# One change to the chunked recurrence of a hybrid decoder block: three short groups of products per chunk become one

## The chip, the core and the metric

The kernel runs on one core of a Trainium2 chip. The metric is device time in microseconds (us) of one execution; a profiled execution leaves a trace with the start and length of every instruction. PE is the matrix engine (TensorE), PEld its weight loads, DVE the vector engine, ACT the scalar engine, POOL the GpSimd engine, SP the queue that issues most DMA transfers.

## The reference

One decoder layer over 512 tokens with width 1024. An input projection feeds a sparse-attention mixer, an RWKV-7 mixer and two gates; both mixers are projected and merged, and a gated MLP follows. The change is about the RWKV-7 recurrence, which the reference writes as a scan over tokens, for 8 heads with a 64 x 64 state each:

```python
def step(state, inp):
    r_t, w_t, k_t, v_t, a_t, b_t = inp
    sa = jnp.einsum('bhij,bhj->bhi', state, a_t)
    state = state * w_t[:, :, None, :] + sa[..., None] * b_t[:, :, None, :] + v_t[..., None] * k_t[:, :, None, :]
    return state, jnp.einsum('bhij,bhj->bhi', state, r_t)
...
mean = jnp.mean(y, axis=-1, keepdims=True)
var = jnp.mean(jnp.square(y - mean), axis=-1, keepdims=True)
y = (y - mean) * lax.rsqrt(var + GN_EPS) * ln_g.reshape(H, N) + ln_b.reshape(H, N)
y = y + jnp.sum(r * k * r_k, axis=-1, keepdims=True) * v
return y.reshape(b, s, RWKV_WIDTH) * g
```

Two further parts are touched: the columns of the input projection that make the gates (`sigmoid(gate_a)`, `sigmoid(gate_b)`), and the compression MLP of the attention mixer, whose last product gives `vc`.

## The kernel before

**The recurrence in chunks.** The 512 tokens are cut into `NCH` = 8 chunks of `C` = 64. Heads are held in pairs: `p` counts 4 pairs, `r` the two heads of a pair, in the lower and upper 64 partitions. The loop over `c` (L930) works out, for each chunk:

- `X`, a PSUM bank: the chunk's own term (`x_own`, L917, eight products on a 64 x 64 tile of the array) plus `AR . M0`, the state's part (eight products, L935). `Xs` is its copy to SBUF (L941, DVE).
- `U` (L946): eight products of `AB` with `Xs`. Two copies put it into `UV`: ACT the lower partitions (L947), DVE the upper (L948).
- `Mp` (L957): eight products of `BKT` with `UV`, on a 128 x 64 tile. Two DVE operations add it to the state and scale it by `PC`, giving `M1`, the state of the next chunk.
- `Y`, the output: `AR . M0` (L939, 64 x 64) and `AB . UV` (L968, 128 x 64). ACT copies it to `Ys`; every second chunk, `group_norm` (L849) normalizes two chunks' `Ys` on DVE and ACT, then turns it with transposes on PE, multiplies it with a gate product (`gg`), and puts the result into `BO`.

So `X` to `Xs` to `U` to `UV` to `Mp` is a chain with two hops through DVE and ACT. Each small fp32 product appears in the trace as two matmul records, so eight products read as x16.

**The dense products between.** The generator `fill_chain` (L875) holds other work for PE. One `next(fill)` is one step: 12 of the 24 matmuls of a dense product with 128 columns of weights (`dense_fm_g`, L400: 8 x 2 with the weights' high part `whi` against the activations' two parts `hh` and `hl`, then 8 with the low part `wlo`), or a piece of the compression MLP (`compress`, L784), or one token block of a K/V projection (`kv1`). The loop calls it three times per chunk: after `Xs`, after `UV`, and at the end (L942, L952, L987), and once ahead of the loop. The products for gate A are called GA1 to GA7 here, those for gate B GB0 to GB6.

**Weights.** `wload` (L260) has SP fetch a 512 KB tile into one of three `raw` buffers. `wsplit_` (L277) makes the high part on ACT (L292) and the low part on the engine that `weight_tiles` (L213) names (L294): DVE for most, POOL for some. `whi` and `wlo` have two buffers each, and a `raw` buffer is fetched into again when its low part has been made. The two weight tiles of each piece of the compression MLP use `raw` buffers directly, until PE has read them.

**Order.** PE's order in the recurrence is the program's (`manual_schedule` with PE). The order on ACT, DVE, POOL and SP comes from a planner which runs ahead of time, and each of these engines then takes its instructions strictly in that order. A product that reads or writes a PSUM bank and a copy that reads the same bank are kept apart, by tile.

Of the kernel before, what the change touches and what calls it, by code (L numbers as in the profile page):

```python
# [10 lines left out]
F32 = mybir.dt.float32  # L11
# [3 lines left out]
ALU = mybir.AluOpType  # L15
# [8 lines left out]
DH = 64  # L24
H = 8
NH2 = H // 2
C = 64
NCH = S // C
# [52 lines left out]
def hybrid_block(ctx: ExitStack, tc: tile.TileContext, A: dict, out: bass.AP):  # L81
    nc = tc.nc
    v, sc, te = nc.vector, nc.scalar, nc.tensor
# [19 lines left out]
    def close(cm):  # L103
        cm.__exit__(None, None, None)
# [8 lines left out]
    def pa():  # L113
        return bank("a", 2)
# [4 lines left out]
    def mm(o, l, r, start, stop):  # L119
        te.matmul(o, lhsT=l, rhs=r, start=start, stop=stop)  # L120

    def act(o, i, f=AF.Copy, **kw):
        sc.activation(o, i, f, **kw)  # L123

    def tt(o, a, b, op):
        v.tensor_tensor(o, a, b, op=op)  # L126
# [45 lines left out]
    def cols(name):  # L172
        r0, n = ROWS[name]
        return prm[:, r0:r0 + n]
# [38 lines left out]
    def weight_tiles():  # L213
        def cols(w, o, kt=KT, eng=v):
            return w[:, o:o + 128], kt, 128, eng

        def rows(w, o, n, kt=KT, eng=v):
            step = 1024 // n
            for i, k0 in enumerate(range(0, kt, step)):
                kn = min(step, kt - k0)  # L220
                yield w[128 * k0:128 * (k0 + kn), o:o + n], kn, n, eng[i] if type(eng) is list else eng

        pool_ = nc.gpsimd
        yield cols(w_in, O_RWKV + 1536, eng=pool_)
        yield cols(w_in, O_RWKV + 1664, eng=pool_)
        for p in range(NH2):
            for o in (512, 0, 1024):
                yield cols(w_in, O_RWKV + o + 128 * p)
        yield cols(w_in, O_KC)
        yield from rows(w_in, O_Q, 512, eng=[v, pool_, ("spare", pool_), v])  # L230
        yield cols(w_in, O_VC)
        yield from rows(w_in, O_KS, 256, eng=[v, ("spare", v)])
        for m in range(NGA):
            yield cols(w_in, O_GA + 128 * m)
        yield from rows(w_in, O_KW, 280, eng=pool_)
        for m in range(NGA, KT):
            if m < 4:
                for s4 in range(m if m > NGA else 0, m + 1):
                    for s_ in "kv":
                        yield A["cmp_w1_" + s_][0][512 * s4:512 * s4 + 512], 4, 256, None  # L240
            yield cols(w_in, O_GA + 128 * m)
        for m in range(NGB):
            yield cols(w_in, O_GB + 128 * m)
        for m in range(KT):
            if m + NGB < KT:
                yield cols(w_in, O_GB + 128 * (m + NGB), eng=pool_ if m else v)
            yield cols(A["w_proj_b"][0], 128 * m, NH2, eng=pool_)
        for m in range(KT):
            yield cols(A["w_proj_a"][0], 128 * m, NH2)
        yield from rows(A["w_out"][0], 0, 512)  # L250
        yield from rows(A["w_out"][0], 512, 512, eng=())
        for f in range(NF):
            yield cols(A["w_up"][0], DFF + 128 * f)
            yield cols(A["w_up"][0], 128 * f)
        for hf in range(2):
            yield from rows(A["w_down"][0], 512 * hf, 512, NF)
# [136 lines left out]
    def run(g):  # L393
        while True:
            try:
                next(g)
            except StopIteration as e:
                return e.value

    def dense_fm_g(xh, xl, kt=KT):  # L400
        hi, lo = wnext(kt, 128)
        p = mmb()
        for k in range(kt):
            mm(p, hi[:, k], xh[:, k], k == 0, False)
            mm(p, hi[:, k], xl[:, k], False, False)
            if 4 * k == 3 * kt - 4:
                yield
        for k in range(kt):
            mm(p, lo[:, k], xh[:, k], False, k == kt - 1)
        return p  # L410
# [373 lines left out]
    def compress():  # L784
# [43 lines left out]
        for g in range(2):  # L828
            for e in range(2):
                bs = slice(64 * g + 32 * e, 64 * g + 32 * e + 32)  # L830
                for m in range(2):
                    mm(kc_ps[bs, 128:192], hidT[:, m, 1, 32 * g:32 * g + 32], cw2[:, 1, m], m == 0, m == 1)
                act(vcb[bs, 2 * g + e], kc_ps[bs, 128:192], AF.Copy, scale=0.5)
        for g in range(2):
            act(kcd[:, g, 0], kc_ps[0:32, 64 * g:64 * g + 64], AF.Copy, scale=0.5)
# [39 lines left out]
    def fill_chain():  # L875
        cp_ = compress()
        next(cp_)
        next(kv1)
        yield
        next(cp_)  # L880
        yield from kv1
        ts(gts, gts, 0.25, 0.25)
        yield
        for m in range(NGA, KT):
            next(cp_, None)
            act(siga[m], (yield from dense_fm_g(hh, hl)))
            yield
        assert next(cp_, 0) == 0
        for m in range(NGB):
            act(tb[m], (yield from dense_fm_g(hh, hl)))  # L890
            yield

# [21 lines left out]
    def hsl(r, n=64):  # L914
        return slice(64 * r, 64 * r + n)
# [6 lines left out]
                   c == 0 and p == NH2 - 1)  # L922


    with tc.manual_schedule(engines={mybir.EngineType.PE}):
        M0 = Ys = gn = None
        X = pb()
        x_own(0, X)
        next(fill, None)
        for c in range(NCH):  # L930
            Y = pa()
            if M0 is not None:
                for p in range(NH2):
                    for r in range(2):
                        mm(X[hsl(r), 64 * p:64 * p + 64], AR[hsl(r), p, c, 0, :], M0[hsl(r), p, :], False,  # L935
                           p == NH2 - 1)
                for p in range(NH2):
                    for r in range(2):
                        mm(Y[hsl(r), 64 * p:64 * p + 64], AR[hsl(r), p, c, 1, :], M0[hsl(r), p, :], p == 0, False)  # L939
            Xs = tp.tile([128, NH2, DH], F32, name="Xs", tag="Xs", bufs=2)  # L940
            v.tensor_copy(Xs, X[:, 0:256].rearrange("p (a d) -> p a d", d=DH))  # L941
            next(fill, None)  # L942
            U = pb()
            for p in range(NH2):
                for r in range(2):
                    mm(U[hsl(r), 64 * p:64 * p + 64], AB[hsl(r), c, p, r, 0:64], Xs[hsl(r), p], True, True)  # L946
            act(UV[0:64, c, :, 0, :], U[0:64, 0:256].rearrange("p (a d) -> p a d", d=DH))  # L947
            v.tensor_copy(UV[64:128, c, :, 1, :], U[64:128, 0:256].rearrange("p (a d) -> p a d", d=DH))  # L948
            if c < NCH - 1:
                X = pb()  # L950
                x_own(c + 1, X)
            next(fill, None)  # L952
            if c < NCH - 1:
                Mp = pa()
                for p in range(NH2):
                    for r in range(2):
                        mm(Mp[hsl(r), 64 * p:64 * p + 64], BKT[:, c, p, r, :], UV[:, c, p, r, :], True, True)  # L957
                M1 = tp.tile([128, NH2, DH], F32, name="M", tag="M", bufs=2)
                mpv = Mp[:, 0:256].rearrange("p (a d) -> p a d", d=DH)
                pc = PC[:, :, c:c + 1].to_broadcast([128, NH2, DH])  # L960
                if M0 is None:
                    tt(M1, mpv, pc, ALU.mult)
                else:
                    tt(M1, M0, mpv, ALU.add)
                    tt(M1, M1, pc, ALU.mult)
            for p in range(NH2):
                for r in range(2):
                    mm(Y[hsl(r), 64 * p:64 * p + 64], AB[:, c, p, r, 64:128], UV[:, c, p, r, :],  # L968
                       M0 is None and p == 0, p == NH2 - 1)
            if c % 2 == 0:  # L970
                Ys = tp.tile([128, H, DH], F32, name="Ys", tag="Ys", bufs=2)
            for r in range(2):
                act(Ys[hsl(c % 2), r::2, :], Y[hsl(r), 0:256].rearrange("p (h d) -> p h d", d=DH))
            if c % 2 == 1:
                gn = group_norm(c - 1, Ys)
                if c < NCH - 1:
                    next(gn)
            M0 = M1
            if 4 <= c < 6:
                for a in range(4 * c - 16, 4 * c - 12):  # L980
                    bias_rows(a)
            if c == NCH - 2:
                bias_compressed()
            if c == NCH - 1:
                for h0 in range(0, H, 4):
                    act(BT[:, h0:h0 + 4, 0:256], BT[:, h0:h0 + 4, 256:257].to_broadcast([128, 4, 256]))
            next(fill, None)  # L987
            if gn is not None and c % 2 == 0:
                run(gn)
                gn = None  # L990
    close(rp_cm)


# [383 lines left out]
```

## Time and profile before

| | us |
|---|---|
| median of 3 runs | 848.09 (847.67 to 848.52) |
| the profiled execution | 847.76 |
| its span, first to last instruction | 846.0 |
| busy: PE, PEld, DVE, ACT, POOL | 831.9, 676.2, 514.7, 405.7, 52.5 |
| the recurrence on PE, from x_own(0) to the last copy to Ys | about 180 to 288 |

In the timeline each row has the start (us from the span's start), the length, the engine, the line, the operation, the tiles (out<-in), the tile of the array or the shape, and the count of merged instructions. In brackets stand the engine's idle time before the row and what ended it. L120 is the line of the helper that issues every matmul, L123 that of every ACT operation. "128*128", "64*64" and "128*64" are the part of the array that a product uses. The end of a matmul is modelled, so the pace is read from start to start.

### The profile page before, as it was taken

The numbers are of one execution on the slowest core, as the hardware profiler recorded it, in microseconds if no ns is written. First come the engines' busy times: TensorE is split into PE (matmuls) and PEld (weight loads), VectorE is DVE, ScalarE is ACT, GpSimd is POOL, SyncE is SP. The second block draws the span as 40 slices with busy tenths as digits, with TensorE's granted clock in tenths as the row PEclk, the third lists the DMA queues.
The fourth block names the chain that finished last, engine by engine and source line by source line (L and its number), as shares of the span: only waits on it lengthen the run. The fifth ranks groups of instructions, "written<-read, shape, count | busy, mean of one in ns | idle before, by whom it ended". The sixth has DMA issues, their size and how long they took to land.

```text
span 846.0 us, 12844 instructions
## 1 busy us (share of the span) xinstructions
PE 831.9 (98%) x5097; PEld 676.2 (80%) x5097; DVE 514.7 (61%) x998; ACT 405.7 (48%) x784; POOL 52.5 (6%) x69
## 2 busy tenths in 40 slices
PE   7999999999999999999999999999999999999998
PEld 6777778897777886777788888888888888888886
DVE  5477779963555678888675566666666666322222
ACT  6766645443545677767344454444444444221210
POOL 6200020140000110111000000000000000000000
PEclk9999999999999999999999999999999999999999
DMA  7432222335551320010167023333333332333421
GB/s 231 112 86 62 75 75 76 92 108 151 132 119 50 83 69 13 15 36 26 52 215 221 0 77 98 100 100 100 100 100 95 90 91 98 100 100 112 136 75 50
DMA packets 109104, 78.73 MB, mean 93 GB/s; under 512 B 3869, under 2 KB 97748, under 8 KB 109044
## 3 DMA queue, kind: packets, MB, share of 16 engines
q1 hardware_dynamic: 106512, 73.51, 29.8%
q0 software_dynamic: 1472, 1.86, 1.0%
q10 hardware_dynamic: 1060, 2.55, 1.0%
q8 instruction: 40, 0.66, 0.3%
q14 instruction: 20, 0.16, 0.1%
HBM read 74.56 MB, written 2.29 MB: 91 GB/s over the span
## 4 chain that ended last, share of the span: by engine, by line
PE 52%; DVE 0%; ACT 0%; DVEq 0%; issue 0%
PE ps_mm L120 52%; DVE hl L135 0%; PE ps_a L120 0%; PE ps_b L1181 0%; PE ps_a L200 0%; PE ps_mm L1181 0%; ACT hh L123 0%; PE ps_b L200 0%; DVE x L126 0%; DVEq L1373 0%; PE ps_a L1133 0%
## 5 line engine op out<-in xcount | busy, mean ns | idle before, releaser
L294 DVE TENSOR_TENSOR wlo<-raw,whi 128x1024 fp32r<-128x1024 f32 (+1 forms) x111 | 131.6, 1185 | 189.4 <-PE ps_mm L120 166.8
L120 PE MATMUL ps_mm<-hh,whi 128*128 128x512 f32 (+1 forms) x624 | 243.3, 392 | 0.4 <-ACT hh L123 0.3
L120 PE MATMUL ps_mm<-hl,whi 128*128 128x512 f32 (+1 forms) x624 | 240.9, 388 | 0.3 <-DVE hl L135 0.2
L123 ACT ACTIVATE whi<-raw 128x1024 fp32r<-128x1024 f32 (+3 forms) x124 | 123.4, 996 | 170.3 <-PE ps_mm L120 142.4
L120 PE MATMUL ps_mm<-hh,wlo 128*128 128x512 f32 (+1 forms) x624 | 151.8, 385 | 0.0
L120 PEld LDWEIGHTS ps_mm<-hh,whi 128*128 128x128 f32 x624 | 117.3, 188 | 27.3 <-issue 1.3
L120 PEld LDWEIGHTS ps_mm<-hl,whi 128*128 128x128 f32 x624 | 117.4, 188 | 24.1 <-DVE hl L135 1.0
L120 PEld LDWEIGHTS ps_mm<-hh,wlo 128*128 128x128 f32 x624 | 115.2, 188 | 23.3
L120 PE MATMUL ps_mm<-whi,aT 128*128 128x512 f32 x352 | 84.5, 390 | 0.0
L120 PEld LDWEIGHTS ps_mm<-whi,aT 128*128 128x128 f32 x352 | 65.9, 188 | 14.3 <-issue 0.4
L135 DVE SCALAR_TENSOR_TENSOR cgv<-ps_mm,cw,cgv 128x511 f32<-128x511 f32 (+1 forms) x88 | 65.4, 746 | 1.5
L123 ACT ACTIVATE cgv<-ps_mm,cw 128x512 f32<-128x512 f32 x44 | 34.3, 781 | 22.8 <-PE ps_mm L120 22.8
L120 PE MATMUL ps_mm<-wlo,aT 128*128 128x512 f32 x176 | 44.3, 390 | 0.0
L123 ACT ACTIVATE P<-P,nm 128x512 f32<-128x512 f32 (+3 forms) x64 | 35.4, 554 | 14.9 <-DVE nm L1155 14.9
L123 ACT ACTIVATE aT<-cgv 128x512 fp32r<-128x512 f32 x22 | 13.9, 631 | 56.8 <-DVE cgv L126 56.8
L120 PEld LDWEIGHTS ps_mm<-wlo,aT 128*128 128x128 f32 x176 | 33.1, 188 | 6.9
L123 ACT ACTIVATE cgv<-cgv 128x512 f32<-128x512 f32 x22 | 13.9, 632 | 43.9 <-DVE cgv L135 43.8
L294 POOL TENSOR_TENSOR wlo<-raw,whi 128x512 fp32r<-128x512 f32 (+3 forms) x13 | 20.4, 1573 | 203.6 <-PE ps_mm L120 147.9
L1155 DVE CUSTOM_DVE_ANT_0 P<-ps_a,AB 128x512 f32<-128x512 f32 (+3 forms) x64 | 29.4, 484 | 4.2 <-PE ps_a L120 3.7
L126 DVE TENSOR_TENSOR x<-x,ps_mm 128x512 f32<-128x512 f32 (+1 forms) x17 | 11.1, 656 | 23.9 <-PE ps_mm L120 22.7
L126 DVE TENSOR_TENSOR aT<-cgv,aT 128x512 fp32r<-128x512 f32 x22 | 15.2, 693 | 14.7 <-ACT aT L123 14.7
L120 PE MATMUL ps_a<-KH,qst 128*128 128x512 f32 (+3 forms) x64 | 21.3, 349 | 1.5 <-DVE nm L1155 0.9
(356 smaller groups left out, 1205.5 us busy)
## 6 DMA issues: line engine op xcount, KB each, us to landing
raw<-in_w_up_dram SPq DMA_DIRECT2D x44, 512.0 KB, 3.8
raw<-in_w_in_dram SPq DMA_DIRECT2D x38, 512.0 KB, 3.9
raw<-in_w_down_dram SPq DMA_DIRECT2D x22, 512.0 KB, 3.6
raw<-in_w_out_dram SPq DMA_DIRECT2D x8, 512.0 KB, 3.7
xt<-in_x_dram SPq DMA_DIRECT2D x4, 512.0 KB, 5.7
raw<-in_cmp_w_k_dram SPq DMA_DIRECT2D x4, 512.0 KB, 4.0
raw<-in_cmp_w_v_dram SPq DMA_DIRECT2D x4, 512.0 KB, 4.4
raw<-in_w_proj_b_dram SPq DMA_DIRECT2D x8, 256.0 KB, 2.7
```

What stands on the lines that cost most here:

```text
L120: te.matmul(o, lhsT=l, rhs=r, start=start, stop=stop)
L123: sc.activation(o, i, f, **kw)
L126: v.tensor_tensor(o, a, b, op=op)
L135: v.scalar_tensor_tensor(o, a, s, b, op0=op0, op1=op1)
L294: eng.tensor_tensor(lo, raw, hi.bitcast(F32), op=ALU.subtract)
L1155: v.tensor_tensor_reduce(out=P[:, i], in0=sp[:, N * (i - i0):N * (i - i0) + N], in1=BT[:, h, 384 - 128 * qt:512], scale=-1.0, scalar=-NEG, ...
```

## The change

- In the loop, the output of chunk c-1 (`outputs`, new) is computed in chunk c, in two halves: the state's part and two head pairs between `X` and `U`, the other two pairs between `U` and the own term of the next chunk. The last chunk's output follows its own `U`.
- `x_own` of the next chunk and `Mp` follow directly; only then come the chunk's three steps of `fill`, in one stretch. In chunk 0 one step stays between `Xs` and `U`, in place of the one ahead of the loop.
- `Xs` is copied in two halves of two pairs each, one by DVE, one by ACT.
- `group_norm` of chunks c-2 and c-1 starts in the even chunk c ahead of the stretch, and its transposes follow the stretch.
- The low parts of GA1 to GA7 and GB0 to GB6 are made on POOL in place of DVE (14 tiles).
- In `compress`, the eight products for `vc` are issued together and their four copies (`vcb`) after them, where each pair of products was followed by its copy.
- A check that `compress` has ended is made one product later.

```diff
-            yield cols(w_in, O_GA + 128 * m)
+            yield cols(w_in, O_GA + 128 * m, eng=pool_)
         for m in range(NGB):
-            yield cols(w_in, O_GB + 128 * m)
+            yield cols(w_in, O_GB + 128 * m, eng=pool_)
...
                 for m in range(2):
                     mm(kc_ps[bs, 128:192], hidT[:, m, 1, 32 * g:32 * g + 32], cw2[:, 1, m], m == 0, m == 1)
+        for g in range(2):
+            for e in range(2):
+                bs = slice(64 * g + 32 * e, 64 * g + 32 * e + 32)
                 act(vcb[bs, 2 * g + e], kc_ps[bs, 128:192], AF.Copy, scale=0.5)
...
-        assert next(cp_, 0) == 0
         for m in range(NGB):
+            if m == 1:
+                assert next(cp_, 0) == 0
...
+    def outputs(c, M):
+        Y = pa()
+        for p in range(NH2 if M is not None else 0):
+            for r in range(2):
+                mm(Y[hsl(r), 64 * p:64 * p + 64], AR[hsl(r), p, c, 1, :], M[hsl(r), p, :], p == 0, False)
+        for p in range(NH2):
+            if p == 2:
+                yield
+            for r in range(2):
+                mm(Y[hsl(r), 64 * p:64 * p + 64], AB[:, c, p, r, 64:128], UV[:, c, p, r, :], M is None and p == 0,
+                   p == NH2 - 1)
+        for r in range(2):
+            act(Ys[c // 2][hsl(c % 2), r::2, :], Y[hsl(r), 0:256].rearrange("p (h d) -> p h d", d=DH))
...
-            v.tensor_copy(Xs, X[:, 0:256].rearrange("p (a d) -> p a d", d=DH))
-            next(fill, None)
+            v.tensor_copy(Xs[:, 0:2], pairs(X)[:, 0:2])
+            act(Xs[:, 2:4], pairs(X)[:, 2:4])
+            if c == 0:
+                next(fill, None)
+            else:
+                if c % 2 == 1:
+                    Ys[c // 2] = tp.tile([128, H, DH], F32, name="Ys", tag="Ys", bufs=2)
+                yc = outputs(c - 1, Mp0)
+                next(yc)
             U = pb()
...
+            Mp0 = M0
+            if c:
+                run(yc)
             if c < NCH - 1:
                 X = pb()
                 x_own(c + 1, X)
-            next(fill, None)
-            if c < NCH - 1:
                 Mp = pa()
...
+                M0 = M1
+            else:
+                run(outputs(c, Mp0))
...
-            next(fill, None)
-            if gn is not None and c % 2 == 0:
+            if c and c % 2 == 0:
+                gn = group_norm(c - 2, Ys[c // 2 - 1])
+                next(gn)
+            for i in range(3):
+                next(fill, None)
+            if gn is not None:
                 run(gn)
                 gn = None
+        gn = group_norm(NCH - 2, Ys[NCH // 2 - 1])
```

More of the change, by code (lines that the diff above doesn't have):

```diff
@@ L922, in x_own, with pairs @@
                    c == 0 and p == NH2 - 1)
+    def outputs(c, M):
[11 more added lines that the diff above has]
+            act(Ys[c // 2][hsl(c % 2), r::2, :], Y[hsl(r), 0:256].rearrange("p (h d) -> p h d", d=DH))
+    def pairs(ap):
+        return ap[:, 0:256].rearrange("p (a d) -> p a d", d=DH)
     with tc.manual_schedule(engines={mybir.EngineType.PE}):
-        M0 = Ys = gn = None
+        M0 = M1 = gn = None
+        Ys = {}
         X = pb()
         x_own(0, X)
-        next(fill, None)
         for c in range(NCH):
-            Y = pa()
             if M0 is not None:
@@ L936, in hybrid_block @@
                            p == NH2 - 1)
-                for p in range(NH2):
-                    for r in range(2):
-                        mm(Y[hsl(r), 64 * p:64 * p + 64], AR[hsl(r), p, c, 1, :], M0[hsl(r), p, :], p == 0, False)
             Xs = tp.tile([128, NH2, DH], F32, name="Xs", tag="Xs", bufs=2)
-            v.tensor_copy(Xs, X[:, 0:256].rearrange("p (a d) -> p a d", d=DH))
-            next(fill, None)
+            v.tensor_copy(Xs[:, 0:2], pairs(X)[:, 0:2])
[7 more added lines that the diff above has]
+                next(yc)
             U = pb()
@@ L946, in hybrid_block @@
                     mm(U[hsl(r), 64 * p:64 * p + 64], AB[hsl(r), c, p, r, 0:64], Xs[hsl(r), p], True, True)
-            act(UV[0:64, c, :, 0, :], U[0:64, 0:256].rearrange("p (a d) -> p a d", d=DH))
-            v.tensor_copy(UV[64:128, c, :, 1, :], U[64:128, 0:256].rearrange("p (a d) -> p a d", d=DH))
+            act(UV[0:64, c, :, 0, :], pairs(U)[0:64])
+            v.tensor_copy(UV[64:128, c, :, 1, :], pairs(U)[64:128])
+            Mp0 = M0
+            if c:
+                run(yc)
             if c < NCH - 1:
@@ L958, in hybrid_block @@
                 M1 = tp.tile([128, NH2, DH], F32, name="M", tag="M", bufs=2)
-                mpv = Mp[:, 0:256].rearrange("p (a d) -> p a d", d=DH)
                 pc = PC[:, :, c:c + 1].to_broadcast([128, NH2, DH])
                 if M0 is None:
-                    tt(M1, mpv, pc, ALU.mult)
+                    tt(M1, pairs(Mp), pc, ALU.mult)
                 else:
-                    tt(M1, M0, mpv, ALU.add)
+                    tt(M1, M0, pairs(Mp), ALU.add)
                     tt(M1, M1, pc, ALU.mult)
[L966 to L978, printed above, removed]
+                M0 = M1
+            else:
+                run(outputs(c, Mp0))
             if 4 <= c < 6:
@@ L986, in hybrid_block @@
                     act(BT[:, h0:h0 + 4, 0:256], BT[:, h0:h0 + 4, 256:257].to_broadcast([128, 4, 256]))
-            next(fill, None)
-            if gn is not None and c % 2 == 0:
+            if c and c % 2 == 0:
[4 more added lines that the diff above has]
+            if gn is not None:
                 run(gn)
                 gn = None
+        gn = group_norm(NCH - 2, Ys[NCH // 2 - 1])
     close(rp_cm)
```

## The prediction

> **What bounds the kernel now.** I read the page first, then the chain that ended last, then the timeline of each engine in the recurrence.
>
> ```profile
> span 846.0 us, 12844 instructions
> PE 831.9 (98%) x5097; PEld 676.2 (80%) x5097; DVE 514.7 (61%) x998; ACT 405.7 (48%) x784; POOL 52.5 (6%) x69
> PE 52%; DVE 0%; ACT 0%; DVEq 0%; issue 0%
> ```
>
> PE is busy 98% of the span, and the chain that ended last runs over PE alone. So DVE time that moves to POOL gains nothing by itself. What counts is the sum of PE's issue times and of PE's waits. A busy PE still loses time when it changes the part of the array it uses:
>
> ```profile
> 195.34 0.39 PE L120 MATMUL ps_mm<-hh,whi 128*128 128x512 f32 x1
> 195.57 0.39 PE L120 MATMUL ps_mm<-hl,whi 128*128 128x512 f32 x1
> 195.89 0.68 PE L120 MATMUL ps_b<-M,AR 64*64 64x64 f32 x16
> 196.41 0.63 PE L120 MATMUL ps_a<-M,AR 64*64 64x64 f32 x16
> 196.97 0.50 PE L120 MATMUL ps_mm<-hh,whi 128*128 128x512 f32 x1
> 197.31 0.39 PE L120 MATMUL ps_mm<-hl,whi 128*128 128x512 f32 x1
> ...
> 210.19 0.63 PE L120 MATMUL ps_a<-M,AR 64*64 64x64 f32 x16
> 210.75 1.95 PE L120 MATMUL ps_mm<-raw,sg 128*64 128x256 f32 x16
> ...
> 283.04 0.68 PE L120 MATMUL ps_b<-Xs,AB 64*64 64x64 f32 x16
> 283.65 0.50 PE L120 MATMUL ps_mm<-hh,whi 128*128 128x512 f32 x1
> ```
>
> Dense matmuls follow each other every 0.23 (195.34 to 195.57). One group of 16 records lasts 0.61 to the next shape (283.04 to 283.65), two lasted 1.08 (195.89 to 196.97), so 16 records cost 0.47 in steady flow and the boundary about 0.14: 0.05 in the first 16 (0.52) and 0.09 in the last (0.56). Into a short group PE loses 0.09 more (0.32 against 0.23), and the first dense matmul behind it 0.11 (0.34 against 0.23). A short group between dense stretches thus costs 0.34 beyond its work. The pair at 210.19 is the important one: a change from 64*64 to 128*64 takes the same 0.56 as a change back to dense. I price every inner change of shape at 0.14.
>
> [...]
>
> **Part 1, shapes: +0.2.** Before, chunks 1 to 7 have three short groups each: 3 x 0.34 = 1.02. After, there is one group, but inside it X and the output's state part (64*64), output (128*64), U (64*64), output, own term, Mp alternate: five changes, 0.34 + 5 x 0.14 = 1.04. The saving of two boundaries is eaten. Chunk 0 falls from two groups (0.68) to one with a single change (0.48), -0.20. Pieces of the compression MLP that used to touch a short group move: four weight pieces cost 0 or 0.14 at a touch, 0.34 alone; two gain a neighbour, two lose one, about +0.05, and the last transposes lose theirs, +0.20. With 7 x 0.02 this gives +0.2. Bounds: -4.7 if inner changes were free (7 x 5 x 0.14 = 4.9 less), +0.6.
>
> **Part 2, vcb copies behind all products: -1.4.**
>
> ```profile
> 238.44 0.86 PE L120 MATMUL ps_mm<-QK 128*32 128x64 f32 x12
> 239.60 0.41 PE L120 MATMUL ps_mm<-QK 128*32 128x64 f32 x4 [0.30 <-ACT kc L123]
> 240.32 0.41 PE L120 MATMUL ps_mm<-QK 128*32 128x64 f32 x4 [0.30 <-ACT kc L123]
> 241.03 0.41 PE L120 MATMUL ps_mm<-QK 128*32 128x64 f32 x4 [0.30 <-ACT kc L123]
> ```
>
> Twelve records last 0.86 with a tail near 0.2, so about 0.06 each, and four need 0.24. With the wait for the copy, a group takes 0.72 (239.60 to 240.32). Three waits of 0.47 go; the products run through. The bracket says 0.30 because ends of matmuls are modelled.
>
> **Part 3, the hops.** Today every copy of the recurrence hides behind 12 dense matmuls, 2.8 us. Then about 1 us of short products hides it. The copies:
>
> ```profile
> 183.14 0.28 ACT L123 ACTIVATE QK<-ps_mm 128x128 f32<-128x128 f32 x1 [1.39 <-PE ps_mm L120]
> 188.42 0.43 DVE L948 COPY UV<-ps_b 64x256 f32<-64x256 f32 x1 [6.50 <-ACT UV L123]
> 196.62 0.42 DVE L941 COPY Xs<-ps_b 128x256 f32<-128x256 f32 x1 [1.28 <-PE ps_b L120]
> 245.09 0.38 ACT L123 ACTIVATE UV<-ps_b 64x256 f32<-64x256 f32 x1 [2.55 <-PE ps_b L120]
> ```
>
> DVE's half of UV waited for ACT's half: two copies from one bank run one after the other. The UV hop is therefore 0.22 (a group's tail: 0.68 of rows against 0.46 of starts) + 0.38 + 0.43 + three handovers of 0.05 = 1.2. Its cover in chunks 1 to 6 is two pairs' output (0.24 + 0.14), the own term (0.61) and the change ahead of them (0.14), 1.1: no stall above 0.1 while ACT and DVE are free. Xs, in halves of about 0.28, likewise needs 0.6 for its first half and 0.9 for its second, against a cover of 1.1 and 1.3 (in chunk 1, with no state's part yet, 0.6 and 0.8).
>
> [...]
>
> Stalls where they are not free, or the cover is short:
>
> - Chunk 0, UV hop: the cover is the own term alone, 0.61 against 1.2: +0.6 (0.4 to 0.9, ACT also copies a K/V block then).
> - Chunk 0, loads. The stretch there follows the first weight piece directly.
>
> ```profile
> 184.91 0.40 PE L120 MATMUL ps_mm<-whi,hh 128*128 128x280 f32 x1
> 187.05 0.51 PE L120 MATMUL ps_b<-Xs,AB 64*64 64x64 f32 x10
> 191.08 1.90 PE L120 MATMUL ps_mm<-raw,sg 128*64 128x256 f32 x16
> 192.91 0.50 PE L120 MATMUL ps_mm<-hh,whi 128*128 128x512 f32 x1
> 185.47 0.46 SPq L265 DMA_DIRECT2D raw<-in_w_in_dram  x1
> 190.60 1.06 ACT L123 ACTIVATE whi<-raw 128x1024 fp32r<-128x1024 f32 x1 [1.98 <-DMA raw<-in_w_in_dram]
> ```
>
> The piece ends at 184.91; its buffers let GA1's load start at 185.47, and whi is ready at 191.66, 6.75 later. Without the short groups PE has two K/V blocks (2 x 2.14) and a piece (1.83) ahead of GA1: 6.1. Stall +0.6 (0 to 1.2).
>
> - Chunk 2, the order on ACT: +1.5.
>
> ```profile
> 202.70 0.50 PE L120 MATMUL ps_mm<-hh,whi 128*128 128x512 f32 x1
> 204.60 0.45 SPq L265 DMA_DIRECT2D raw<-in_w_in_dram  x1
> 210.25 1.06 ACT L123 ACTIVATE whi<-raw 128x1024 fp32r<-128x1024 f32 x1 [2.64 <-DMA raw<-in_w_in_dram]
> ...
> 216.75 1.06 ACT L123 ACTIVATE whi<-raw 128x1024 fp32r<-128x1024 f32 x1 [3.37 <-DMA raw<-in_w_in_dram]
> 218.02 0.36 ACT L123 ACTIVATE UV<-ps_b 64x256 f32<-64x256 f32 x1
> 219.44 1.09 PE L120 MATMUL ps_a<-UV,BKT 128*64 128x64 f32 x15
> ```
>
> The planner puts whi ahead of copies and expects its load sooner than it lands: ACT stood 2.64 and 3.37 at such a whi, UV went behind it, and PE's group at 219.44 (1.09 against 0.68) paid 0.3 even behind dense cover. That stall goes, -0.3, as GA4's load then ends inside a stretch. But GA3's whi begins 7.55 after GA2's first matmul and ends at 8.6. After the change GA2's 24 matmuls end after 5.7, chunk 2's X follows at once, and ACT's half of Xs is due at 6.8. Behind whi it is done at 8.9, while U wants it at 7.4: +1.5. Bounds 0 (planner puts the copy first) to 2.1 (GA2's own bank copy, 0.6, goes first as well).
>
> - Chunks 3, 5, 7, the normalization's end:
>
> ```profile
> 225.15 1.50 ACT L123 ACTIVATE o<-ps_a,prm 128x128 f32<-128x128 f32 x4 [3.29 <-PE ps_a L867]
> 225.26 0.68 PE L120 MATMUL ps_b<-M,AR 64*64 64x64 f32 x16
> 227.41 0.69 DVE L126 TENSOR_TENSOR BO<-o,ps_b 128x512 f32<-128x512 f32 x1
> ```
>
> Its four ACT copies and its DVE operations meet X, now without dense cover. ACT's half of Xs waits until 1.4 after X starts and is just in time. The last DVE operation ends 2.85 after X starts; it holds the gate's bank, which the next own term may need, and UV's copy (due at 2.6) stands behind it. Stall 0.3 each, +1.0 (0 to 2).
>
> **Part 4, low parts on POOL: 0.**
>
> ```profile
> 118.42 2.35 POOL L294 TENSOR_TENSOR wlo<-raw,whi 128x1024 fp32r<-128x1024 f32 x1 [90.62 <-PE ps_mm L120]
> 191.69 1.23 DVE L294 TENSOR_TENSOR wlo<-raw,whi 128x1024 fp32r<-128x1024 f32 x1 [0.44 <-ACT whi L123]
> 300.26 0.51 POOL L1019 DMA_DIRECT2D KL<-KL  x1 [1.43 <-DVE rs_y L135]
> 310.54 0.39 PE L120 MATMUL ps_a<-KH,qst 128*128 128x512 f32 x1
> ```
>
> 1.1 slower each, but wlo is read only 16 matmuls (3.7) into its product. It frees raw 1.1 later and delays GA2's load: counted from GA1's first matmul, low part 2.4, load 5.1 (185.47 to 190.60) and whi 1.06 end at 8.6, and GA2 comes after half of GA1 (2.9), the short group (96 records, 2.8, and 1.04), the rest (2.8) and a piece (1.8): 11.3. POOL also issues the key transfers, the last 10 us ahead of their first use, so a low part of 2.35 fits in front. What the move is worth is that no 1.23 stands on DVE ahead of Xs or UV. The moved check does nothing.
>
> **Sum.** +0.2 - 1.4 - 0.3 + 0.6 + 0.6 + 1.5 + 1.0 = +2.2 on the profiled execution's 847.76 (span 846.0 and 1.76 around it): 850.0. That execution lies 0.33 under the median, so 850.3 against 848.09.
>
> **Rivals.**
> - *The hops stay covered.* If the planner puts every copy ahead of whi, and the normalization slips past, 1.5 and 1.0 fall away: -0.3, 847.8. For it: the covers of 1.1 to 1.3 fit free engines. Against: the rows at 216.75.
> - *Faster: inner changes of shape are free.* Part 1 becomes -4.7 and the sum -2.7: 845.4. It decides once a change costs below about 0.03 (a sum of -1.7). The row at 210.19 is against it; only 128*64 to 64*64 is unseen.
> - *Late weights hold up chunk 1 as well.* GA2's whi comes ahead of chunk 1's UV on ACT. By part 4 it runs from 7.5 to 8.6 after GA1's start; UV's copy is due near 4.8 (2.9, X 0.61, output 0.38, U 0.61 and a tail): +3.8, 854.1. It decides if the planner expects the load within 2.4 of its issue (4.8 less the low part's 2.4).
> - *It does not do what it says*: the moved low parts could leave DVE busy at the hops all the same, with what the row at 227.41 shows. That is the stall of chunks 3, 5, 7 at its upper bound, 851.3, inside the forecast's own range.
>
> **Chances and range.** Forecast (849.4 to 852) 0.48; covered hops (847 to 849.3) 0.28; free changes 0.10; late weights 0.14. 0.2% is 1.7 us, about what a measurement of this kernel tells from no change. Faster by more: 0.10 and a little of the covered case, 0.13. Within: most of that case and the low edge of the forecast, 0.33. Slower: 0.54. The range leaves out half of the faster case and half of the late one: 846.0 to 854.1; the forecast's own is 849.4 to 852.
>
> **What would show it.** Right: at 64*64 to 128*64 boundaries inside the group 0.56 for 16 records; no ACT waits at the vcb products; idle PE in chunk 0 ahead of Mp and of GA1; a whi with a DMA wait on ACT just before an Xs copy in chunk 2; PE waiting ahead of Mp in chunks 3, 5, 7. Wrong: a short group of chunks 4 or 6 much longer than 3.9 (96 records and 1.04), stalls that grow chunk by chunk, or a change after 300 us.

## The result and the profile after

The changed kernel takes 860.9 us (median of 5 runs, 858.66 to 863.44), the kernel before 847.97 beside it (847.53 to 848.52): 1.0157 times as long, with a 95% interval of 1.014 to 1.0175. The forecast was 850.3. It had the sign and the mechanisms of most terms; of the loss of 12.9 us its sum had 2.2. Part of the spread is PE's granted clock: over the execution it has a mean of 0.994 in the two longest runs (863.44 and 861.91) and of 0.998 in the other three.

The page of the changed kernel:

```profile
span 859.1 us, 12852 instructions
PE 834.6 (97%) x5097; PEld 680.3 (79%) x5097; DVE 506.2 (59%) x984; ACT 409.3 (48%) x792; POOL 85.9 (10%) x83
```

DVE is 8.5 us less busy than before and POOL 33.4 more; PE is idle 24.5 us (859.1 - 834.6) instead of 14.1 (846.0 - 831.9). The first key product, the end of the stretch that the change touches, shows where the time went (timeline of PE):

```profile
323.68 0.39 PE L120 MATMUL ps_a<-KH,qst 128*128 128x512 f32 x1
```

Before, this row stood at 310.54. The whole 13.1 are lost ahead of it. What PE waited for from 176 to 320 (the view of waits: total, times, longest):

```profile
PE ps_a L870 <- DVE Ys L126: 5.1, 2, 4.4
PE ps_mm L847 <- DVE QK L130: 2.6, 2, 2.3
PE ps_b L120 <- ACT Xs L123: 1.5, 1, 1.5
PE ps_mm L120 <- ACT whi L123: 0.7, 1, 0.7
PE ps_a L120 <- ACT UV L123: 0.4, 1, 0.4
PE ps_b L120 <- DVE BO L126: 0.2, 1, 0.2
```

Together 10.5; the kernel before waited 0.9 ahead of the same row, for the copies of `vcb`. The two largest, 7.7, are waits for DVE's normalization and for the compression MLP's normalization of keys: neither is in the forecast. Behind the longest one, the first row below (timeline of PE), PE also ran slower. The second row is the view by stretches: the stretch, its length, the busy time of PE, PEld, DVE, ACT and POOL, the granted clock, the DMA share and GB/s:

```profile
230.88 0.34 PE L870 MATMUL ps_a<-kc,Ys 128*128 128x128 f32 x1 [4.38 <-DVE Ys L126]
```

```profile
231.00:234.42 3.42, 3.42 (x29) 3.19 (x29) 0.00 (x0) 1.23 (x4) 0.00 (x0) 0.50 0.49 143
```

By estimate, 3.4 us at half the clock are 1.7 lost; 16 records took 0.91 there (233.50 to 234.41), against 0.52 at 1.00 (246.25 to 246.77). The 9.6 more of waits and this 1.7 make 11.3 of the 13.1. The rest was not traced: short delays and the changes of shape add to it, and the vcb copies take from it.

**Why DVE was late: POOL.** DVE's and POOL's rows ahead of the wait, two views in the order of time:

```profile
223.16 0.69 DVE L860 TENSOR_REDUCE n<-sq 128x8 f32<-128x512 f32 x1 [4.93 <-ACT sq L123]
223.76 1.48 DVE L132 TENSOR_SCALAR QK<-QK 128x256 f32<-128x256 f32 x1
...
227.10 0.17 DVE L135 SCALAR_TENSOR_TENSOR n<-rs_y,n 128x8 f32<-128x8 f32 x1
227.30 2.31 DVE L126 TENSOR_TENSOR rs_y<-n 128x8 f32<-128x8 f32 x1
...
230.04 0.69 DVE L126 TENSOR_TENSOR Ys<-Ys,n 128x512 f32<-128x512 f32 x1
```

```profile
222.69 2.41 POOL L294 TENSOR_TENSOR wlo<-raw,whi 128x1024 fp32r<-128x1024 f32 x1 [6.63 <-ACT whi L123]
227.25 2.34 POOL L294 TENSOR_TENSOR wlo<-raw,whi 128x1024 fp32r<-128x1024 f32 x1 [2.15 <-ACT whi L123]
```

An operation on 8 columns, 0.17 long at 227.10, takes 2.31 at 227.30 and ends at 229.61, with POOL's low part (229.59). The one at 223.76 ends at 225.24, POOL's at 225.10. The reduction at 223.16 ran beside POOL in its usual 0.69. The two delayed ones read SBUF and write SBUF; copies out of PSUM beside a low part kept their length (Xs at 246.98, 0.29, with POOL busy from 246.46 to 248.82). The kernel before already had one such pair, which the prediction passed over (its timelines of DVE and of POOL):

```profile
177.32 1.34 DVE L126 TENSOR_TENSOR rs_y<-kss 128x8 f32<-128x8 f32 x1
```

```profile
177.22 1.41 POOL L294 TENSOR_TENSOR wlo<-raw,whi 128x560 fp32r<-128x560 f32 x1 [6.33 <-ACT AB L123]
```

**And the order on ACT.** ACT's rows of chunk 2 and of the normalization:

```profile
212.56 1.06 ACT L123 ACTIVATE whi<-raw 128x1024 fp32r<-128x1024 f32 x1 [7.81 <-DMA raw<-in_w_in_dram]
213.52 0.58 ACT L123 ACTIVATE sg<-ps_mm 128x512 f32<-128x512 f32 x1
214.00 0.27 ACT L123 ACTIVATE Xs<-ps_b 128x128 f32<-128x128 f32 x1
...
221.55 1.06 ACT L123 ACTIVATE whi<-raw 128x1024 fp32r<-128x1024 f32 x1 [5.56 <-DMA raw<-in_w_in_dram]
222.51 0.61 ACT L123 ACTIVATE sq<-Ys 128x512 f32<-128x512 f32 x1
```

Twice a whi stood at the head of ACT until its load landed. The first held up Xs, as forecast, together with the copy of GA2's bank behind it (sg, 213.52). The second held up the squares of the normalization until 222.51, so that the reduction behind them began at 223.16, inside POOL's low part.

### The profile page after: what moved, and what is told of

Same layout as the page of the kernel before. It is cut to its first block, busy times and chain, and to the rows that moved or that the text cites. A ratio compares the mean times of both kernels' runs of the same rounds, so it can differ in the third digit from the quotient of the medians.

```text
span 859.1 us, 12852 instructions
## 1 busy us (share of the span) xinstructions
PE 834.6 (97%) x5097; PEld 680.3 (79%) x5097; DVE 506.2 (59%) x984; ACT 409.3 (48%) x792; POOL 85.9 (10%) x83
## 4 chain that ended last, share of the span: by engine, by line
PE 52%; DVE 0%; ACT 0%; DVEq 0%; issue 0%
PE ps_mm L120 51%; DVE hl L135 0%; PE ps_a L120 0%; PE ps_b L1201 0%; PE ps_a L200 0%; PE ps_mm L1201 0%; ACT hh L123 0%; PE ps_b L200 0%; DVE x L126 0%; DVEq L1393 0%; PE ps_a L1153 0%
## 5 line engine op out<-in xcount | busy, mean ns | idle before, releaser
L294 DVE TENSOR_TENSOR wlo<-raw,whi 128x1024 fp32r<-128x1024 f32 (+1 forms) x97 | 114.5, 1180 | 172.3 <-PE ps_mm L120 160.4
L294 POOL TENSOR_TENSOR wlo<-raw,whi 128x1024 fp32r<-128x1024 f32 (+3 forms) x27 | 53.9, 1995 | 291.6 <-PE ps_mm L120 203.1
L959 DVE COPY Xs<-ps_b 128x128 f32<-128x128 f32 x8 | 2.3, 289 | 38.1 <-PE ps_b L120 38.1
## 6 DMA issues: line engine op xcount, KB each, us to landing
raw<-in_w_proj_b_dram SPq DMA_DIRECT2D x8, 256.0 KB, 2.7
```

The source lines that it names most:

```text
L294: eng.tensor_tensor(lo, raw, hi.bitcast(F32), op=ALU.subtract)
L959: v.tensor_copy(Xs[:, 0:2], pairs(X)[:, 0:2])
```

## The experiments

Every median stands beside runs of the kernel before on the same chip; the ratio to those has its 95% interval in brackets.

### Low parts

**All back on DVE.** The changed kernel with

```diff
-            yield cols(w_in, O_GA + 128 * m, eng=pool_)
+            yield cols(w_in, O_GA + 128 * m)
-            yield cols(w_in, O_GB + 128 * m, eng=pool_)
+            yield cols(w_in, O_GB + 128 * m)
```

> The changed kernel with its 14 low parts back on DVE; all else as changed. Theory P (a DVE operation with two SBUF inputs, or an SBUF-to-SBUF scalar operation, that meets a POOL low part waits until that one ends): no 128x8 DVE operation above 0.3 us is left, the stall ahead of the transposes of the compressed keys (2.5 us at 259.4) goes, the one ahead of the first normalization's transposes (4.4 at 230.9) falls to 1 to 3 because the squares still stand behind a weight tile's high part on ACT; a new low part of 1.23 stands ahead of Xs in chunks 2, 4, 6, up to 0.8 each. 852 to 856 against 860.9. Rival R (the single stretch itself leaves the normalization too little time, whoever makes the low parts): the stalls stay, 858 to 862.

Measured 854.78, 1.0084 (1.0071 to 1.0098). The low parts on POOL thus cost 6.1 of the 12.9. The wait for the normalization is gone; its last operation ended at 224.71 instead of 230.73. The other waits:

```profile
PE ps_b L120 <- DVE Xs L959: 1.9, 1, 1.9
PE ps_mm L120 <- ACT whi L123: 0.7, 1, 0.7
PE ps_mm L847 <- DVE QK L130: 0.5, 2, 0.3
PE ps_b L120 <- DVE BO L126: 0.4, 2, 0.2
PE ps_a L120 <- ACT UV L123: 0.4, 1, 0.4
```

GA4's whi on ACT (timeline of the same run):

```profile
218.03 1.06 ACT L123 ACTIVATE whi<-raw 128x1024 fp32r<-128x1024 f32 x1 [1.43 <-DMA raw<-in_w_in_dram]
```

Chunk 2 still waits, now for DVE's half of Xs, behind GA3's low part. GA4's whi is done waiting 3.5 earlier than in the changed kernel (218.03 against 221.55): low parts that take 2.4 instead of 1.23 also free the raw buffers later. GA4's load is issued as GA3's low part ends, at 216.09 in the changed kernel and at 214.19 here, and whi could start 5.5 and 3.8 after that. So POOL acted in two ways: by the delays of DVE operations shown above (0.17 became 2.31) and through the loads.

**On POOL in the kernel before.** Its own loop, with `eng=pool_` in the same two lines of `weight_tiles`.

> The kernel before with only the 14 low parts moved to POOL. Theory P: DVE operations of 128x8 or 32x2 of over 1 us appear while POOL makes a low part, and PE waits where it needs what stands behind them (the normalization's transposes, the compressed keys): 850 to 854 against 848. Rival R: POOL's low parts are read late and hidden, 847.7 to 848.7.

Measured 851.36, 1.0047 (1.0032 to 1.0062): +3.5, in the range of theory P. The move costs time without the stretch too, but not at the transposes that this theory named. PE waited for copies on ACT (view of waits):

```profile
PE ps_a L120 <- ACT UV L123: 1.3, 1, 1.3
PE ps_mm L120 <- ACT whi L123: 1.2, 2, 0.8
```

GA4's whi waits for its load until 220.41 there, until 216.75 in the kernel before, and ACT's half of UV stands behind it. In the old loop it is thus mostly the later load that shows at PE.

**In four pieces.** The changed kernel, each such low part on POOL as four instructions:

```diff
+            if eng is nc.gpsimd and kt == 8 and n == 128:
+                for q in range(0, kt, 2):
+                    eng.tensor_tensor(lo[:, q:q + 2], raw[:, q:q + 2], hi[:, q:q + 2].bitcast(F32), op=ALU.subtract)
+            else:
+                eng.tensor_tensor(lo, raw, hi.bitcast(F32), op=ALU.subtract)
```

> The changed kernel with each POOL low part of 128x1024 made in four instructions of 128x256 (about 0.65 each). Theory P in the form that a DVE operation waits for the end of the POOL instruction that runs, and then goes first: no DVE operation waits over 0.7, the stalls at 230.9 and 259.4 shrink by 1.5 to 2 each, 856 to 858. P in the form that POOL's next piece takes its turn between two DVE operations: a chain of small DVE operations waits for all four pieces one by one, 860 to 862 with many DVE operations of 0.6 to 0.8. Rival R: no change in any DVE length, 860 to 862.

Measured 857.13, 1.0108 (1.0094 to 1.0122): 3.8 back. DVE beside the four pieces, which POOL made from 226.29 to 229.09:

```profile
226.44 0.62 DVE L135 SCALAR_TENSOR_TENSOR n<-rs_y,n 128x8 f32<-128x8 f32 x1
227.09 0.66 DVE L126 TENSOR_TENSOR rs_y<-n 128x8 f32<-128x8 f32 x1
```

No delay here lasted longer than a piece, now 0.7, and the engines took turns: the chain of short operations met a piece at each step. The time is that of the expectation's first form, the rows are those of its second.

**GA4 and GA5 alone on DVE** (`eng=v if m in (4, 5) else pool_`): the two low parts that hit the normalization go, GA4's load stays late.

> The changed kernel with the low parts of GA4 and GA5 alone on DVE; the other ten stay on GpSimd. In the changed kernel these two run at 222.69 and 227.25 and DVE's short operations at 223.76 (1.48) and 227.30 (2.31) end with them, ahead of the 4.5 us wait for the normalization. GA3's low part stays on GpSimd, so GA4's load stays late (whi at 221.6). [...]

**GA2 and GA3 alone on DVE** (`eng=v if m in (2, 3) else pool_`): the load is early, the two low parts stay.

> The changed kernel with the low parts of GA2 and GA3 alone on DVE. They end about 1.1 us earlier after their whi, raw buffers come free earlier, and GA4's load with them (its whi stood until 218.0 on ACT with all low parts on DVE, until 221.6 in the changed kernel). GA4's and GA5's low parts stay on GpSimd and still meet the chain. [...] Theory B (late load): the wait falls to 1.5 or less, 857 or less.

Measured 858.78, 1.0131 (1.0117 to 1.0145), and 859.66, 1.0141 (1.0125 to 1.0156). The first run's waits, then the second's:

```profile
PE ps_mm L847 <- DVE QK L130: 2.6, 2, 2.3
PE ps_a L870 <- DVE Ys L126: 1.8, 2, 1.1
PE ps_b L120 <- ACT Xs L123: 1.8, 1, 1.8
```

```profile
PE ps_mm L847 <- DVE QK L130: 2.6, 2, 2.3
PE ps_b L120 <- DVE Xs L959: 2.4, 1, 2.4
PE ps_a L870 <- DVE Ys L126: 0.7, 1, 0.7
```

Without POOL's delays of these DVE operations the wait of 4.4 falls to 1.1; with an early load (whi waits until 218.64) it is gone (the 0.7 is at a later normalization), as the chain then meets one low part only, for 1.04 at its start. Either mechanism taken away removes most of this wait, so it needs both. The second run has the wait of its theory B, but not its time, and the intervals of both runs overlap that of the changed kernel, so it is the waits that decide here. The time fell by less than this wait because the wait for Xs grew and PE ran slower elsewhere, in and behind the wait for the compression chain (view by stretches, the first run):

```profile
254.45:261.28 6.83, 6.00 (x16) 4.67 (x17) 1.02 (x3) 0.83 (x2) 0.45 (x1) 0.50 0.48 97
```

By the same estimate, the 6.0 busy at half the clock are 3.0 lost. The second run lost 1.7 twice, at 0.50 from 215.0 to 218.4 and from 256.0 to 259.4. In the changed kernel the clock stayed at 1.00 from 259 to 265, behind the same wait of 2.3. Waits and clock together are 12.2 in the changed kernel, 10.7 and 10.6 in these two; their profiled executions are 1.5 and 2.1 shorter than its.

### Which engine holds the hop

**Xs on DVE alone**, then **the squares on DVE alone**, then **Xs, both halves of UV and the squares on DVE**, low parts on POOL:

```diff
-            v.tensor_copy(Xs[:, 0:2], pairs(X)[:, 0:2])
-            act(Xs[:, 2:4], pairs(X)[:, 2:4])
+            v.tensor_copy(Xs, pairs(X))
...
-        act(sq, Ys, AF.Square)
+        tt(sq, Ys, Ys, ALU.mult)
...
-            act(UV[0:64, c, :, 0, :], pairs(U)[0:64])
+            v.tensor_copy(UV[0:64, c, :, 0, :], pairs(U)[0:64])
```

> The changed kernel with one edit: the whole of Xs is copied by DVE, as before, instead of half by DVE and half by ACT. In the changed kernel PE waits 1.66 us at 214.32 for ACT's half, which stands behind a whi whose DMA is late. Theory A (that wait is a loss of its own): it goes, no other stall grows by as much, 859.2 (858.3 to 860.0). Theory B (the time until the normalization's end at 230.0 is set by GpSimd and the loads, not by PE): PE only reaches the transposes at 230.9 earlier and waits there that much longer, about 6 instead of 4.5 us; 860.5 to 861.5.

> The changed kernel with one edit: the normalization's squares are made on DVE instead of ACT, where they stood 3.4 us behind the late whi of GA4 (221.55). GpSimd's low parts stay. [...] Theory B (low parts on GpSimd delay DVE's chain wherever it stands): at least 859.

> The changed kernel with ACT taken out of the hops: Xs, both halves of UV and the normalization's squares on DVE; low parts stay on GpSimd. With Xs alone on DVE the wait only moved from Xs to ACT's half of UV (1.9 at 215.95), with the squares alone it stayed at Xs (2.2 at 214.76). Theory A (ACT, which stands at the late whi of GA3 in chunk 2, is what the hop waits for, whichever copy it has): no wait over 0.3 in chunk 2, no lower granted clock there; left are the waits for the normalization (about 3) and the compression chain (about 2.4): 855 (853 to 857). Theory B (the hops wait as long on DVE, as copies that meet GpSimd's low parts): 859 or more.

Measured 861.5, 1.0166 (1.0142 to 1.0189); 857.22, 1.0113 (1.0098 to 1.0128); 858.36, 1.0124 (1.0111 to 1.0138). The first and the third don't come to the time of their theory A, nor the second to that of its theory B. The first has the time of its theory B, but not by the wait which that theory named: PE waited 3.4 for the normalization, against 5.1 in the changed kernel. The wait at Xs only moved to the next copy on ACT; PE's row:

```profile
215.95 1.08 PE L120 MATMUL ps_a<-UV,BKT 128*64 128x64 f32 x15 [1.71 <-ACT UV L123]
```

In the second run the squares were done by 219.4, but the chain's next step stood on DVE behind an operation of the compression MLP, whose input stood on ACT behind the same late whi; PE waited 2.9 for the normalization. In the third run the wait in chunk 2 is gone, as its theory A said of it, and PE waited longer at the next place instead (view of waits):

```profile
PE ps_a L870 <- DVE Ys L126: 5.5, 2, 4.8
```

The clock there was 0.50 from 228.7 to 235.6. So a copy that changed engines moved a wait of chunk 2 to whoever was next behind the late whi, and part of what PE gained there it lost again at the normalization, whose end POOL and the load set (229.35 here, 230.73 in the changed kernel).

### Cover and room

**Cover put back.** Half a dense product again behind Xs and behind the own term, with low parts on DVE and on POOL:

```diff
                 yc = outputs(c - 1, Mp0)
                 next(yc)
+                next(fill, None)
...
                 x_own(c + 1, X)
+                next(fill, None)
...
             else:
+                next(fill, None)
                 run(outputs(c, Mp0))
...
-            for i in range(3):
+            for i in range(1 if c else 2):
                 next(fill, None)
```

> The changed kernel with the low parts back on DVE (854.8) and, as a second edit, a half dense product put back behind Xs and behind the own term in every chunk, so that each hop has its 12 dense matmuls again; outputs stay one chunk late, the normalization too. Theory A (the loss that is left at 854.8 is the missing cover of the hops): 848.5 (847.0 to 850.0): three short groups per chunk again and 3 inner changes of shape more, 7 x 3 x 0.14 = 2.9, on the 845.8 of the kernel before with the vcb copies moved. Theory B (the late outputs and the late normalization cost the time, whatever stands between the hops): 853 to 855.

> As the run with the cover put back, but with the low parts on GpSimd as in the changed kernel. Theory A (GpSimd's low parts hold up DVE in any order, and what it costs depends on the cover): 3 to 4 above the run with low parts on DVE, as in the kernel before (851.4 against 847.8), so 851 to 853. Theory B (the full 6 us are lost wherever the low parts are on GpSimd): 854 or more. Theory C (cover hides it): within 1 of the run with low parts on DVE.

Measured 859.85, 1.0131 (1.0109 to 1.0154), and 869.07, 1.0257 (1.0241 to 1.0272): slower than without cover. The first is above both of its theories; the second lies in its theory B (854 or more), 9.2 above the first. The edit has a second effect that was not meant: one half product is left between the normalization's start and its transposes, which the loop runs at the end of the same chunk. What PE waited for in the first run:

```profile
PE ps_a L870 <- DVE Ys L126: 7.1, 3, 3.5
```

**Room for the normalization.** Its transposes one chunk later, alone on the changed kernel, and with the cover for low parts on DVE and on POOL:

```diff
-            if gn is not None:
+            if gn is not None and c % 2 == 1:
                 run(gn)
                 gn = None
```

> The changed kernel with one edit: each normalization's transposes stand one chunk later in TensorE's order, at the end of the next odd chunk's stretch, so that its chain on ACT and DVE has about 12 us instead of 8.4, as before the change; low parts stay on GpSimd. Theory A (the chain is slowed by GpSimd and by the late whi, but the wait exists only because the change left it one stretch): the waits of 4.5 and 0.9 ahead of the transposes go, with the lower clock behind the first, 854 (852.5 to 855.5). Theory B (PE waits elsewhere for what DVE is late with): 858 or more.

> As the run with the cover put back and low parts on DVE (859.9), but the normalization's transposes also one chunk later: in that run half a dense product alone stood between the normalization and its transposes, and PE waited 8.0 for them in three places. Theory A (hops without cover and a normalization without room are the whole loss): 849.5 (848 to 851), no wait over 0.7. Theory B (outputs one chunk late cost the time themselves): 853 or more.

> As the run before it (cover and room), with low parts on GpSimd. Theory A (GpSimd delays DVE in any order, and raw buffers come free later): 3 to 4 above that run, as in the kernel before (851.4 against 847.8). Theory B (the full 6 us of the changed kernel): 5 or more above. Theory C (with cover and room it hides): within 1.

Measured 858.43, 1.0119 (1.0103 to 1.0134); 851.84, 1.0042 (1.003 to 1.0055); 858.87, 1.0132 (1.0116 to 1.0147). Room alone gives 2.5, not 7, theory B of that run: there is no wait for the transposes any more, but DVE is still as late as in the changed kernel, and its next copy for the recurrence stands behind the same operations (view of waits, here and for POOL with cover and room below):

```profile
PE ps_b L120 <- DVE Xs L959: 2.8, 1, 2.8
```

In and behind that wait the clock was 0.50 from 231.0 to 237.8. With cover and room and low parts on DVE, 851.84 is 8.0 under the run without room, 0.8 above theory A's range and below theory B's. On POOL it is 7.0 more again, theory B of that run; the cover did not hide POOL:

```profile
PE ps_b L120 <- DVE M L126: 3.6, 1, 3.6
```

The cover and the room together are worth 2.9 (854.78 to 851.84), none of it at the normalization's transposes, for which PE didn't wait at 854.78. And 851.84 is still 6.0 over the old loop with the vcb copies moved (845.82, next). By the price of Part 1 the seven chunks' three inner changes account for 2.9; the waits ahead of the first key product are 1.5 (0.8, 0.5 and 0.2), 1.0 more than there (0.5). About 2.1 stay without an owner.

### The vcb copies

**Alone on the kernel before**: only the two lines in `compress` that open a second pair of loops, so that the copies follow all products.

> The kernel before with only the copies to vcb moved behind all their products. Three waits of PE of 0.47 go: 846.6 against 848.0 (846.3 to 846.9). Rival: the waits were covered by a later one, 848.0.

Measured 845.82, 0.9974 (0.9964 to 0.9983): 2.0 faster than the kernel before, a little more than expected, and faster than any other kernel here. PE's row:

```profile
238.90 0.92 PE L120 MATMUL ps_mm<-QK 128*32 128x64 f32 x24
```

**With both halves of UV on DVE**, to remove the one wait left at 220.37.

> The kernel before with the vcb copies behind all products (845.8) and both halves of UV copied by DVE. Left in that kernel is one wait of 0.7 at 220.37, where ACT's half of UV stands behind a late whi. Theory (ACT's order is its cause): it goes, 845.2 (844.8 to 845.7). Rival (DVE's own work, 1.23 of a low part and the normalization, holds UV as long): 845.8 or more.

Measured 846.86, 0.9986 (0.9977 to 0.9995): 1.0 slower than without. The rival is right: DVE had a low part and a step of the compression MLP ahead of UV, and then made the two halves in turn, 0.41 and 0.43; PE's wait grew from 0.5 to 1.2.

## Why the prediction was wrong

**The step that failed: Part 4, "low parts on POOL: 0".** It priced the move by when wlo is read and by the instruction's length, and followed the later raw buffer to GA2's load only. It took DVE and POOL for independent: "no 1.23 stands on DVE ahead of Xs or UV". The runs put it at 6.1 in the changed loop, 3.5 in the loop before and 7.0 with cover and room. DVE operations from SBUF to SBUF lasted until POOL's instruction ended (0.17 became 2.31), and GA4's load, which the sum did not follow behind the longer low parts, comes late: its whi starts 3.5 later and holds ACT. How much of the 6.1 belongs to each was not separated.

**Part 3, the normalization.** The sum had the end of it, +1.0, and found nothing at its start. The change starts it one chunk late, and its transposes stay in that same chunk, behind three half products instead of four. With low parts on DVE that room just sufficed; with POOL's delays PE waited 5.1 there. The compression chain likewise: its steps now close up in one stretch, and PE waited 2.6 for it (0.5 with low parts on DVE). The forecast end itself, BO, was 0.2, and small waits for Xs.

**A slower clock behind a wait.** Not in the sum: 1.7 in the changed kernel, by the estimate above (0.50 from 231.00 to 234.42).

**What held.** Chunk 0: 0.4 at UV (forecast 0.6) and 0.7 at GA1 (forecast 0.6), rows:

```profile
184.52 1.08 PE L120 MATMUL ps_a<-UV,BKT 128*64 128x64 f32 x15 [0.42 <-ACT UV L123]
194.03 0.50 PE L120 MATMUL ps_mm<-hh,whi 128*128 128x512 f32 x1 [0.68 <-ACT whi L123]
214.32 0.45 PE L120 MATMUL ps_b<-Xs,AB 64*64 64x64 f32 x8 [1.50 <-ACT Xs L123]
...
246.25 0.68 PE L120 MATMUL ps_b<-M,AR 64*64 64x64 f32 x16
...
247.33 0.45 PE L120 MATMUL ps_a<-UV,AB 128*64 128x64 f32 x8
247.71 0.68 PE L120 MATMUL ps_b<-Xs,AB 64*64 64x64 f32 x16
...
249.94 0.91 PE L120 MATMUL ps_mm<-QK 128*32 128x64 f32 x24
```

Chunk 2: 1.5, by the mechanism forecast, whi with a DMA wait just ahead of Xs. That the size agrees so well is partly luck: whi ended 8.4 behind GA2's first matmul (205.26 to 213.62) instead of 8.6, and GA2's bank copy, which the forecast had in its upper bound alone, went first too. Part 1: the short group of chunk 4 lasts 3.7 (246.25 to 249.94); the forecast's 3.9 has 0.2 at the two ends in it. Eight records from 128*64 to 64*64, the direction without a row in the prediction, take 0.38 (247.33 to 247.71), 0.14 more than the 0.24 of steady flow. So each inner change does cost its part, and the rival of free changes falls. Part 2: the waits are gone, and the edit alone is worth 2.0, not 1.4: the sum took 0.06 for a record, and 24 of them last 0.91 with their tail. The rival of late weights in chunk 1 did not come about, nor did the covered hops; that the change doesn't do what it says is half true, since POOL made DVE wait where it was to relieve it.

**What stays open.** With low parts on DVE the changed kernel is at 854.78, 9.0 over the kernel with the vcb copies alone, where the sum of the other terms has +3.6 (0.2 - 0.3 + 0.6 + 0.6 + 1.5 + 1.0). The waits (3.9 against 0.5) and a clock of 0.50 from 215.2 to 218.6 (1.7) explain 5.1. Short delays that the view of waits leaves out add some: in six chunks U starts 0.1 to 0.2 late behind Xs, 0.9 in all. About 3 have no owner, with cover and room 2.1. No run isolates the one-chunk delay of the outputs.

## What to carry to other kernels

That POOL is idle does not make an operation moved to it free: look in the profile for DVE operations from SBUF to SBUF that overlap a POOL instruction, price the move with up to POOL's full length at each (2.31 at 227.30 here), and follow the buffers that come free later to the loads behind them. When a stretch of other work is taken out between two steps of a chain, ask also which second chain had its room there. The wait removed by moving Xs to DVE returned at the next copy behind the same late instruction (1.71 at 215.95), so the late instruction is what to move.

## What the runs showed of the hardware

- Beside a POOL low part, a DVE operation of 0.17 from SBUF to SBUF lasted until POOL's instruction ended (2.31 at 227.30 in the changed kernel); with POOL's work in pieces of 0.7 the two engines alternated (0.62 at 226.44, 0.66 at 227.09). A TENSOR_SCALAR from SBUF to SBUF waited too (1.48 at 223.76); a TENSOR_REDUCE (0.69 at 223.16) and copies from PSUM (0.29 at 246.98) didn't.
- In the changed kernel PE's granted clock was 0.50 from 231.00 to 234.42, and 1.00 in these three stretches of it (length, then PE's busy time; the clock is third from the end):

```profile
227.59:231.00 3.41, 0.12 (x1) 0.15 (x2) 3.04 (x4) 0.69 (x2) 2.00 (x1) 1.00 0.24 56
254.90:258.31 3.41, 1.89 (x9) 1.16 (x7) 3.41 (x15) 1.58 (x2) 1.63 (x1) 1.00 1.17 139
258.31:261.72 3.41, 2.31 (x10) 1.94 (x11) 1.29 (x3) 0.83 (x2) 0.72 (x1) 1.00 0.71 154
```

The wait of 4.4 leaves PE idle for 3.3 of the first stretch, just ahead of the 0.50. The wait of 2.3 lies across the other two, which have 1.5 and 1.1 idle, and the clock stays at 1.00 to 265. In the kernel with low parts on DVE, whose longest wait is 1.9, PE is idle for 1.9 of this stretch, and behind it the clock is 0.50 from 215.16 to 218.57:

```profile
211.74:215.16 3.42, 1.49 (x40) 1.22 (x34) 1.43 (x2) 2.45 (x4) 0.00 (x0) 1.00 0.01 2
```

So the length of the wait alone did not decide: 1.9 went with a lower clock in one run, and 2.3 with one in the run with GA4 and GA5 on DVE (0.50 from 254.45 to 261.28), but not in the changed kernel. What decides was not shown.
